# A two-layer hybrid transformer block on one core: the keys and queries of layer 2's attention are split a unit sooner, and the context's two attention units move into the small PSUM bank

## The chip, the core and the metric

The kernel runs on one core of a Trainium2 chip. Its time is the device time of one execution in microseconds (us); the median of three runs before is 3200.51 us (3197.03 to 3209.38). Five engines work side by side, each in its own order, and wait for each other through semaphores: TensorE (PE: matmuls and transposes, into the eight banks of PSUM), VectorE (DVE), ScalarE (ACT), GpSimd (POOL) and SyncE (SP), whose queue issues most transfers (DMA).

## The reference

Two layers run over 1024 latent tokens and 256 context tokens. Each layer has a convolution module, a retention part and multi-head attention side by side, one output projection, and a SwiGLU feed-forward part. The change touches attention alone. Shortened, with `l` the layer:

```python
def block_attention(q, k, v):                 # 8 heads, dq = 96, dv = 64
    ...
        s = jnp.einsum('bqhd,bkhd->bhqk', qi, k).astype(jnp.float32) * scale
        p = jax.nn.softmax(s, axis=-1).astype(v.dtype)
        return jnp.einsum('bhqk,bkhd->bqhd', p, v)
...
    attL = block_attention(qmL, jnp.concatenate([kmC, kmL], axis=1), jnp.concatenate([vmC, vmL], axis=1))
    ...
    if not last:
        attC = block_attention(qmC, kmC, vmC)
```

Latent queries (1024) read 1280 keys in both layers. Context queries (256) read the 256 context keys, and only in the first layer.

## The kernel before

**Units.** Attention of a layer is a loop over 8 heads `h` and two blocks `g` of 512 queries, each of four units `a` of 128 queries: 8 units a head, which the text numbers 0 to 7 (unit 8 is unit 0 of the next head). A unit's scores are nine matmuls into `S`, a PSUM tile of three banks of which there are two (`psum(S=2, po=1, mm=1)`): each operand is held as a rounded part and a rest (`kh`, `kl`, `qh`, `ql`), and three products replace one. DVE takes the negated row maximum `nm` (L994), ACT the exponentials `P` with their sums (L999), and DVE transposes `P` in blocks of 32 into `T1` (L1091). After a block's fourth unit, POOL (4 copies, L1026) and SP (12 DMAs, L1024) bring the 32-blocks of `T1` into place as `PT`.

**Weighing.** Five units later PE weighs the values with `PT` in four chunks, one a unit (`weigh_chunk`, L1037, into the bank `po`). With the last chunk it spreads the reciprocal sums over a tile of the one small bank `mm` (L1011), and `normalise` reads `po` and `mm`: two steps on ACT (L1049, L1051), one on DVE (`raw<-po,raw`) and one on POOL (`raw<-raw`).

**Context.** After unit 7 of a head (for the last head after unit 3) of layer 1, `context_units` computes two units of 128 context queries against 256 keys. Both write into one `S` tile, in different banks, each followed by its own maximum; then come two exponentials. A step later PE transposes them into `mm` (`direct_transposes`, L1064), ACT copies them out (L1069), another step later PE weighs them into `mm` (`direct_weigh`, L1075, L1011), and ACT and DVE finish (`od`).

**What sets the order.** The order on every engine is the order of the code. Two counters delay steps: `mids` ticks behind a unit's scores, `steps` at a unit's end; `later(d, f)` runs `f` at the d-th tick from now. What the work of a head needs is prepared during the head before: `load_head` (4 DMAs into the two `kq` tiles), `split_k` (ACT rounds `kh`, L877; POOL subtracts `kl`) and `split_q`, once for each block (`qh` on ACT, `ql` on POOL). Before, `split_k` runs at the end of unit 4, `split_q` of block 0 at the end of unit 5 and of block 1 at the end of unit 7, in both layers. The helper `mms` (L105) issues the products, `tt` (L80) every two-input step, so these go by tile names.

Of the kernel before, what the change touches and what calls it, by code (L numbers as in the profile page):

```python
# [11 lines left out]
F32 = mybir.dt.float32  # L12
# [4 lines left out]
AX = mybir.AxisListType  # L17
# [12 lines left out]
H_MLA = 8  # L30
# [13 lines left out]
def body(tc, I, out):  # L44
    nc = tc.nc
    mult, add, sub = ALU.mult, ALU.add, ALU.subtract

    def pool(name, bufs=1, space=None, side=None):
        kw = {}
        if space is not None:  # L50
            kw["space"] = space
        if side is not None:
            kw["side"] = side
        return tc.tile_pool(name=name, bufs=bufs, reuse_waits="tile", **kw)
# [6 lines left out]
    smp = es.enter_context(pool("small", 4))  # L61
# [14 lines left out]
    def bank(tag="mm", cols=512):  # L76
        return pools[tag].tile([128, cols], F32, name=tag, tag=tag)
# [25 lines left out]
    def mms(ps, xs, start=True, stop=True):  # L103
        for i, (a, b) in enumerate(xs):
            nc.tensor.matmul(ps, lhsT=a, rhs=b, start=start and i == 0, stop=stop and i == len(xs) - 1)  # L105
# [365 lines left out]
    with ExitStack() as st:  # L471
# [25 lines left out]
        A, S = modA[0, 0], modS[0, 0]  # L497
# [12 lines left out]
    for l in range(L):  # L510
        last = l == L - 1
# [453 lines left out]
        def split_wo(hf, kps, p=None):  # L965
            for kp in kps:
                wo_pcs[hf].append(piece(I["w_out"][l, hf, kp], leng=None if kp % 2 else nc.vector, p=p,
                                        raw=wo_raw.pop((hf, kp), None)))
# [15 lines left out]

        def scores(u, ps):

            nk = len(u.kts) * 128
            k0 = u.kts[0] * 128
            for c in range(0, nk, 512):
                n = min(512, nk - c)  # L990
                kc = slice(k0 + c, k0 + c + n)
                mms(ps[:, c:c + n], [(u.qh, u.hd.kh[:, kc]), (u.ql, u.hd.kh[:, kc]), (u.qh, u.hd.kl[:, kc])])
            u.nm = smp.tile([128, 1], F32, name="nm", tag="nm")
            nc.vector.reduce_max(out=u.nm, in_=ps[:, :nk], axis=AX.X, negate=True)  # L994
            u.ps = ps[:, :nk]

        def exponentials(u, P):

            nc.scalar.activation(out=P, in_=u.ps, func=AF.Exp, bias=u.nm, accum_out=u.sm)  # L999
            u.P = P  # L1000
# [87 lines left out]
        steps, mids, soon = Ticks(), Ticks(), []  # L1088
# [5 lines left out]
        def after(u, us, T1):  # L1094

            if T1 is None:
                return
            block_transpose(u, T1)
            if u is not us[-1]:
                return  # L1100
            blocks(us, T1)
            for i in range(len(CHUNKS)):
                mids.later(5 + i, weigh_chunk, us, i)
            steps.later(5, reciprocals, us)

        def late():
            while soon:
                f, *x = soon.pop(0)
                f(*x)

        def context_units(h):
            us = []
            rc = rawp.tile([128, 1024], F32, name="raw", tag="raw")
            ps = bank("S", 1536)
            sums = smp.tile([128, 4], F32, name="sums", tag="sums", bufs=6)
            for a in range(2):
                u = Unit()
                u.h, u.g, u.a, u.hd, u.kts, u.ending = h, 2, a * 128, heads[h], CTX, False
                u.qh, u.ql = (x[:, a * 128:a * 128 + 128] for x in qs[h, 2])
                u.sums, u.sm, u.t = sums, sums[:, a:a + 1], rc[:, 512:]  # L1120
                us.append(u)
                scores(u, ps[:, a * 512:])
            for a, u in enumerate(us):
                exponentials(u, rc[:, a * 256:a * 256 + 256])
            mids.later(1, direct_transposes, us)
            mids.later(2, direct_weigh, us)

        prev = None
        with tc.manual_schedule():
            for ti, (h, g) in enumerate(todo):  # L1130
                if ti == len(todo) - 1:
                    steps.later(E0, load_wo, 0, (0, 1))
                    steps.later(E1, split_wo, 0, (0, 1))
                    steps.later(E2, load_mixed, 0, 0)
                    steps.later(E2, load_mixed, 0, 1)
                    steps.later(E2, load_wo, 0, (2, 3))
                if g == 0:
                    if not last:
                        steps.later(1, split_q, h, 2)
                    if h:  # L1140
                        mids.later(1 if last else 2, load_v, h)
                    else:
                        steps.later(1, split_q, 0, 1)
                    if h < H_MLA - 1:
                        mids.later(1 if last else 2, load_head, h + 1)
                elif g == 1 and h < H_MLA - 1:
                    steps.later(1, split_k, h + 1)
                    steps.later(2, split_q, h + 1, 0)
                    steps.later(4, split_q, h + 1, 1)
                us = []  # L1150
                direct = ti == len(todo) - 1
                T1 = tp_.tile([128, 4, 4, 320], F32, name="T1", tag="T1")
                sums = smp.tile([128, 4], F32, name="sums", tag="sums", bufs=6)
                for a in range(4):
                    u = Unit()
                    u.h, u.g, u.a, u.hd, u.kts, u.ending = h, g, a * 128, heads[h], kvt, ti == len(todo) - 1
                    u.qh, u.ql = (x[:, a * 128:a * 128 + 128] for x in qs[h, g])
                    u.sums, u.sm = sums, sums[:, a:a + 1]
                    us.append(u)
                    if direct:  # L1160
                        P = T1.rearrange("p c u n -> p (c u n)")[:, a * NTOK:a * NTOK + NTOK]
                    else:
                        P = pp_.tile([128, NTOK], F32, name="P", tag="P")
                    scores(u, bank("S", 1536))
                    mids.tick()
                    exponentials(u, P)
                    if prev is not None:
                        after(*prev)
                    late()
                    prev = (u, us, None if direct else T1)  # L1170
                    if direct:
                        u.t = pp_.tile([128, NTOK], F32, name="P", tag="P")
                        mids.later(1 + a, direct_transposes, [u])
                        mids.later(3 + a, direct_weigh, [u])
                    if not last and a == 3 and g == (h < H_MLA - 1):
                        context_units(h)
                    steps.tick()
            while mids.q or steps.q or soon:
                mids.tick()
                late()  # L1180
                steps.tick()
            split_wo(0, (2, 3))
# [21 lines left out]
        def project_out(t, hf):  # L1204
            m_h, m_l = ms[t]
            ps = bank("mm")
            for k in range(KT):
                wh, wl = wo_pcs[hf][k // 2]
                c = slice((k % 2) * 512, (k % 2) * 512 + 512)
                mms(ps, [(m_h[:, k], wh[:, c]), (m_l[:, k], wh[:, c]), (m_h[:, k], wl[:, c])], k == 0, k == KT - 1)  # L1210
                if k % 2:
                    tk.tick()
                if k % 4 == 3:
                    next(todo, None)
            return ps
# [27 lines left out]
        for i, t in enumerate(order):  # L1243
            ps = [firsts.pop(t) if i < 2 else project_out(t, 0), project_out(t, 1)]
# [8 lines left out]
            u = (rawp if late else w2).tile([128, 1024], F32, name="raw" if late else "u", tag="raw" if late else "u")  # L1253
# [104 lines left out]
        steps = {}  # L1358
# [33 lines left out]
        for j in range(NJ):  # L1392
            v = steps.pop(j) if j in steps else first_two(j)
            w, x, u, th1 = v.w, feat.op, v.u, v.th
# [133 lines left out]
        while ahead:  # L1528
# [26 lines left out]
            for t in range(4):  # L1555
                ps = bank("po")
# [34 lines left out]
        for t in tiles:  # L1591
# [4 lines left out]
            ps = [bank("mm") for _ in range(2)]  # L1596
# [123 lines left out]
```

## Time and profile before

| | |
|---|---|
| median of 3 runs | 3200.51 us |
| the profiled execution, its own time | 3198.45 us |
| its span, first to last instruction | 3196.7 us |
| PE, DVE, POOL, ACT busy | 92%, 72%, 47%, 37% of the span |
| attention of layer 1, 446 to 712 us | 266 us, PE busy 234.15 us |
| attention of layer 2, 2130 to 2363 us | 233 us, PE busy 211.31 us |

PE is busy nearly all the time, and what it waits for is named in the view of waits. A row of the timeline gives start, duration, engine, line, operation, tile written and read, and in brackets the idle time of the engine before it with what ended it. A few gaps in a repeated loop are small one by one; they count by their number.

### The profile page before, as it was taken

The numbers are of one execution on the slowest core, as the hardware profiler recorded it, in microseconds if no ns is written. First come the engines' busy times: TensorE is split into PE (matmuls) and PEld (weight loads), VectorE is DVE, ScalarE is ACT, GpSimd is POOL, SyncE is SP. The second block draws the span as 40 slices with busy tenths as digits, with TensorE's granted clock in tenths as the row PEclk, the third lists the DMA queues.
The fourth block names the chain that finished last, engine by engine and source line by source line (L and its number), as shares of the span: only waits on it lengthen the run. The fifth ranks groups of instructions, "written<-read, shape, count | busy, mean of one in ns | idle before, by whom it ended". The sixth has DMA issues, their size and how long they took to land. (4 is left out here: it accounts for less than half of the span.)

```text
span 3196.7 us, 39725 instructions
## 1 busy us (share of the span) xinstructions
PE 2936.5 (92%) x13968; PEld 2271.7 (71%) x13968; DVE 2310.3 (72%) x3254; ACT 1196.4 (37%) x2354; POOL 1489.7 (47%) x1187
## 2 busy tenths in 40 slices
PE   7989989889879999999898898989999899999897
PEld 3667865557768888887776676865568678887675
DVE  4388467767897676655888868468856986666998
ACT  4213545553332222225332513545554332224432
POOL 1274535544432232325774365435644343334993
PEclk9989989999989999999999999999999999999998
DMA  7421157657522322213303421157764332224213
GB/s 278 141 67 34 58 178 182 167 129 255 198 81 98 105 91 91 91 65 138 112 20 109 152 66 48 44 184 178 180 181 155 99 113 86 86 81 154 96 66 119
DMA packets 178527, 381.47 MB, mean 119 GB/s; under 512 B 43255, under 2 KB 77687, under 8 KB 178072
## 3 DMA queue, kind: packets, MB, share of 16 engines
q1 hardware_dynamic: 172980, 360.03, 36.8%
q10 hardware_dynamic: 5348, 18.90, 1.4%
q8 instruction: 111, 1.82, 0.2%
q14 instruction: 88, 0.72, 0.1%
HBM read 242.97 MB, written 76.90 MB: 100 GB/s over the span
## 5 line engine op out<-in xcount | busy, mean ns | idle before, releaser
L80 POOL TENSOR_TENSOR wl<-raw,wh 128x512 fp32r<-128x512 f32 (+2 forms) x208 | 387.3, 1874 | 648.3 <-ACT wh L85 648.1
L85 ACT CAST wh<-raw 128x512 fp32r<-128x512 f32 (+2 forms) x305 | 237.6, 796 | 414.9 <-PE pp L105 190.1
L80 DVE TENSOR_TENSOR w<-pp,w 128x512 f32<-128x512 f32 x308 | 207.4, 686 | 186.2 <-PE pp L105 183.9
L994 DVE TENSOR_REDUCE nm<-S 128x1 f32<-128x1280 f32 (+1 forms) x144 | 196.3, 1363 | 89.4 <-PE S L105 87.9
L105 PE MATMUL po<-wh,gh 128*128 128x512 f32 x504 | 203.0, 403 | 35.8 <-DVE p L80 29.3
L999 ACT ACTIVATE P<-S,nm 128x1280 f32<-128x1280 f32 x120 | 159.4, 1329 | 196.6 <-DVE nm L994 196.6
L1026 POOL COPY PT<-T 32x1280 f32<-32x1280 f32 x120 | 150.0, 1250 | 177.3 <-PE mm L1011 116.6
L80 POOL TENSOR_TENSOR rr<-rv,mh 128x1 f32<-128x1 f32 (+2 forms) x130 | 93.1, 717 | 279.6 <-DVE rv L190 277.3
L105 PE MATMUL po<-wh,gl 128*128 128x512 f32 x504 | 200.1, 397 | 0.0
L105 PE MATMUL po<-wl,gh 128*128 128x512 f32 x504 | 199.5, 396 | 0.0
L584 DVE SCALAR_TENSOR_TENSOR cacc<-cy,cw,cacc 128x1295 f32<-128x1295 f32 (+1 forms) x120 | 193.7, 1655 | 0.0
L80 POOL TENSOR_TENSOR gl<-gr,gh 128x512 fp32r<-128x512 f32 x112 | 172.8, 1567 | 27.5 <-ACT gh L85 27.5
L80 POOL TENSOR_TENSOR wl<-sx,wh 128x1024 fp32r<-128x1024 f32 x44 | 109.5, 2488 | 155.9 <-ACT wh L85 155.9
L1091 DVE STREAM_TRANSPOSE T<-P 128x1280 f32<-128x1280 f32 x120 | 180.0, 1500 | 0.0
L1037 PE MATMUL po<-PT,vr 128*64 128x512 f32 x600 | 161.8, 636 | 9.6 <-POOL PT L1026 2.9
L80 DVE TENSOR_TENSOR raw<-raw 128x512 f32<-128x512 f32 (+1 forms) x96 | 127.5, 1336 | 50.5 <-POOL wl L80 47.6
L105 PE MATMUL S<-kh,qh 96*128 96x512 f32 (+1 forms) x384 | 154.3, 402 | 9.9 <-ACT P L999 8.2
L80 DVE TENSOR_TENSOR p<-p,po 128x512 f32<-128x512 f32 x224 | 145.3, 677 | 16.6 <-PE po L105 16.1
L105 PE MATMUL S<-kh,ql 96*128 96x512 f32 (+1 forms) x384 | 143.0, 372 | 9.2 <-POOL ql L80 9.2
L80 DVE TENSOR_TENSOR wl<-raw,wh 128x512 fp32r<-128x512 f32 (+1 forms) x105 | 125.3, 1202 | 28.0 <-ACT wh L85 27.9
L105 PEld LDWEIGHTS po<-wh,gh 128*128 128x128 f32 x504 | 96.9, 192 | 67.5 <-DVE p L80 34.9
L105 PE MATMUL S<-kl,qh 96*128 96x512 f32 (+1 forms) x384 | 142.6, 371 | 0.0
(437 smaller groups left out, 8703.7 us busy)
## 6 DMA issues: line engine op xcount, KB each, us to landing
PT<-T SPq DMA_DIRECT2D x360, 160.0 KB
raw<-in_mod_w SPq DMA_DIRECT2D x96, 512.0 KB
raw<-in_ffn_in SPq DMA_DIRECT2D x88, 512.0 KB
gd<-w SPq DMA_DIRECT2D x88, 256.0 KB
gr<-gd SPq DMA_DIRECT2D x32, 512.0 KB
xs<-x ACTq DMA_DIRECT2D x28, 512.0 KB
raw<-in_ffn_out SPq DMA_DIRECT2D x28, 512.0 KB
x<-xs SPq DMA_DIRECT2D x26, 512.0 KB
```

Of the source, the lines that this page charges most:

```text
L80: (eng or nc.vector).tensor_tensor(out=out, in0=a, in1=b, op=op)
L85: nc.scalar.copy(h, t)
L105: nc.tensor.matmul(ps, lhsT=a, rhs=b, start=start and i == 0, stop=stop and i == len(xs) - 1)
L584: nc.vector.scalar_tensor_tensor(out=acc[:, ct, :], in0=y0[:, ct, j:j + AW], scalar=w, in1=acc[:, ct, :], op0=mult, op1=add)
L994: nc.vector.reduce_max(out=u.nm, in_=ps[:, :nk], axis=AX.X, negate=True)
L999: nc.scalar.activation(out=P, in_=u.ps, func=AF.Exp, bias=u.nm, accum_out=u.sm)
L1026: nc.gpsimd.tensor_copy(o, i)
L1037: nc.tensor.matmul(u.po[64 * (j % 2):64 * (j % 2) + 64], lhsT=u.hd.v[:, j, :], rhs=src[:, :, j * 32:j * 32 + 32], start=j < 2, stop=j > 7)
L1091: nc.vector.transpose(out=T1[:, :, u.a // 128].rearrange("p c (k i) -> p k c i", i=32), in_=u.P.rearrange("p (k c i) -> p k c i", c=4, i=32))
```

## The change

The context's scores go into `mm` (one bank: 256 columns for each unit) in place of an `S` tile. The six products run without a maximum in between, and one DVE instruction takes both maxima (`nmc`). Context transposes and context weighing come one unit later. In layer 2 `split_k` and both `split_q` come one unit sooner: at the ends of units 3, 4 and 6. In layer 1 they stay at the ends of units 4, 5 and 7; they are only entered in the list earlier.

```diff
         def scores(u, ps):
 
+            score_products(u, ps)
+            nk = len(u.kts) * 128
+            u.nm = smp.tile([128, 1], F32, name="nm", tag="nm")
+            nc.vector.reduce_max(out=u.nm, in_=ps[:, :nk], axis=AX.X, negate=True)
+            u.ps = ps[:, :nk]
+
+        def score_products(u, ps):
             nk = len(u.kts) * 128
             k0 = u.kts[0] * 128
             for c in range(0, nk, 512):
                 n = min(512, nk - c)
                 kc = slice(k0 + c, k0 + c + n)
                 mms(ps[:, c:c + n], [(u.qh, u.hd.kh[:, kc]), (u.ql, u.hd.kh[:, kc]), (u.qh, u.hd.kl[:, kc])])
-            u.nm = smp.tile([128, 1], F32, name="nm", tag="nm")
-            nc.vector.reduce_max(out=u.nm, in_=ps[:, :nk], axis=AX.X, negate=True)
-            u.ps = ps[:, :nk]
...
             rc = rawp.tile([128, 1024], F32, name="raw", tag="raw")
-            ps = bank("S", 1536)
+            ps = bank("mm")
             sums = smp.tile([128, 4], F32, name="sums", tag="sums", bufs=6)
             for a in range(2):
...
                 us.append(u)
-                scores(u, ps[:, a * 512:])
+                u.ps = ps[:, a * 256:a * 256 + 256]
+                score_products(u, u.ps)
+            nm = smp.tile([128, 2], F32, name="nmc", tag="nmc")
+            nc.vector.reduce_max(out=nm, in_=ps.rearrange("p (a k) -> p a k", a=2), axis=AX.X, negate=True)
+            for a, u in enumerate(us):
+                u.nm = nm[:, a:a + 1]
             for a, u in enumerate(us):
                 exponentials(u, rc[:, a * 256:a * 256 + 256])
-            mids.later(1, direct_transposes, us)
-            mids.later(2, direct_weigh, us)
+            mids.later(2, direct_transposes, us)
+            mids.later(3, direct_weigh, us)
...
                     if h < H_MLA - 1:
                         mids.later(1 if last else 2, load_head, h + 1)
-                elif g == 1 and h < H_MLA - 1:
-                    steps.later(1, split_k, h + 1)
-                    steps.later(2, split_q, h + 1, 0)
-                    steps.later(4, split_q, h + 1, 1)
+                        steps.later(4 if last else 5, split_k, h + 1)
+                        steps.later(5 if last else 6, split_q, h + 1, 0)
+                        steps.later(7 if last else 8, split_q, h + 1, 1)
```

**PE in layer 1, between unit 7 and unit 8.** The rows run from the last weighing of unit 7 over the context's six products to the second product of unit 8; the names in brackets are the engines whose semaphores a row waits for. Before:

```order
L1037 MATMUL po<-PT,vr 64x512 x2
L105 MATMUL S<-kh,qch 128x256 [waits Activation_49]
L105 MATMUL S<-kh,qcl 128x256 [waits Pool_49]
L105 MATMUL S<-kl,qch 128x256
L105 MATMUL S<-kh,qch 128x256 [waits DVE_49]
L105 MATMUL S<-kh,qcl 128x256
L105 MATMUL S<-kl,qch 128x256
L105 MATMUL S<-kh,qh 128x512 [waits Activation_49]
L105 MATMUL S<-kh,ql 128x512 [waits Pool_49]
```

And now:

```order
L1041 MATMUL po<-PT,vr 64x512 x2
L105 MATMUL mm<-kh,qch 128x256
L105 MATMUL mm<-kh,qcl 128x256 [waits Pool_49]
L105 MATMUL mm<-kl,qch 128x256
L105 MATMUL mm<-kh,qch 128x256
L105 MATMUL mm<-kh,qcl 128x256
L105 MATMUL mm<-kl,qch 128x256
L105 MATMUL S<-kh,qh 128x512 [waits Activation_49]
L105 MATMUL S<-kh,ql 128x512 [waits Pool_49]
```

The wait for DVE between the two context units is gone, and so is that for ACT ahead of them; the wait for POOL in unit 8's second product stays.

**ACT in layer 1, from unit 8 to unit 10.** `P` is a unit's exponentials, `raw<-po` and `raw<-mm 64x256` are `normalise`, `raw<-mm 128x512` takes the context's transposes out of `mm`, `od<-mm` its weighed values. Before:

```order
L999 ACTIVATE P,sums<-S,nm 128x1280
L1049 COPY raw<-po 64x512
L1051 COPY raw<-mm 64x256 x2
L1069 COPY raw<-mm 128x512
L85 CAST qch<-kq 96x256
L999 ACTIVATE P,sums<-S,nm 128x1280
L1083 COPY od<-mm 64x256
```

And now:

```order
L1003 ACTIVATE P,sums<-S,nm 128x1280
L1053 COPY raw<-po 64x512
L1055 COPY raw<-mm 64x256 x2
L85 CAST qch<-kq 96x256
L1003 ACTIVATE P,sums<-S,nm 128x1280
L1073 COPY raw<-mm 128x512
L1003 ACTIVATE P,sums<-S,nm 128x1280
L1087 COPY od<-mm 64x256
```

The transposes' copy moved behind the exponentials of unit 9, the copy of `od` behind those of unit 10.

**POOL in layer 2, one head.** Before:

```order
L1026 COPY PT<-T_18482 32x1280 x4
L80 TENSOR_TENSOR raw<-raw 64x512
L80 TENSOR_TENSOR kl<-kq,kh 96x1280
L80 TENSOR_TENSOR ql<-kq,qh 96x512 x2
L1026 COPY PT<-T_18594 32x1280 x4
L80 TENSOR_TENSOR raw<-raw 64x512
```

And now:

```order
L80 TENSOR_TENSOR kl<-kq,kh 96x1280
L1030 COPY PT<-T_18466 32x1280 x4
L80 TENSOR_TENSOR raw<-raw 64x512
L80 TENSOR_TENSOR ql<-kq,qh 96x512 x2
L1030 COPY PT<-T_18582 32x1280 x4
L80 TENSOR_TENSOR raw<-raw 64x512
```

`kl` stands ahead of block 0's copies now; both `ql` stay between the blocks. In layer 1 POOL's order is as it was.

## Rows read from the trace of the kernel before

**Rows 1.** Windows: length; busy us of PE, PEld, DVE, ACT, POOL; granted clock; DMA.

```profile
446.00:712.00 266.00, 234.15 (x1120) 148.26 (x1121) 199.17 (x184) 141.47 (x246) 136.14 (x103) 0.94 0.64 157
...
545.51:578.59 33.08, 28.93 (x148) 17.73 (x150) 25.91 (x24) 18.32 (x32) 18.63 (x15) 1.00 0.70 169
578.59:613.59 35.00, 32.17 (x148) 19.27 (x150) 25.91 (x24) 18.32 (x32) 18.65 (x15) 0.90 0.66 160
...
2180.64:2193.01 12.37, 10.49 (x40) 5.66 (x42) 6.58 (x6) 4.73 (x9) 6.78 (x5) 0.72 0.28 65
2299.52:2310.28 10.76, 9.00 (x40) 5.18 (x42) 6.59 (x7) 4.72 (x9) 5.99 (x5) 0.84 0.31 73
2242.80:2251.09 8.29, 7.44 (x38) 4.17 (x38) 6.51 (x7) 4.68 (x9) 4.61 (x5) 1.00 0.31 73
```

**Rows 2.** Waits of PE in layer 1's attention: us in total, times, longest.

```profile
PE S L105 <- DVE nm L994: 14.6, 8, 2.4
PE mm L1064 <- ACT raw L1051: 11.7, 7, 2.2
```

**Rows 3.** Timeline, layer 1, from unit 7 of a head to unit 9.

```profile
566.98 0.39 PE L105 MATMUL S<-kh,qch 96*128 96x256 f32 x1
...
568.05 1.26 POOL L80 TENSOR_TENSOR ql<-kq,qh 96x512 fp32r<-96x512 f32 x1
...
569.35 0.39 PE L105 MATMUL S<-kh,qch 96*128 96x256 f32 x1 [1.75 <-DVE nm L994]
...
570.04 0.39 PE L105 MATMUL S<-kh,ql 96*128 96x512 f32 x1
...
571.62 1.94 PE L1037 MATMUL po<-PT,vr 128*64 128x512 f32 x8
571.73 1.49 DVE L994 TENSOR_REDUCE nm<-S 128x1 f32<-128x1280 f32 x1 [1.29 <-PE S L105]
...
575.37 0.68 DVE L80 TENSOR_TENSOR raw<-po,raw 64x512 f32<-64x512 f32 x1 [0.73 <-ACT raw L1049]
...
576.16 0.66 PE L1064 MATMUL mm<-ident,raw 128*128 128x128 f32 x4 [2.17 <-ACT raw L1051]
576.57 0.47 PE L105 MATMUL S<-kh,qh 96*128 96x512 f32 x1
```

**Rows 4.** Groups by shape, layer 1's attention: busy us, mean ns | idle before.

```profile
L999 ACT ACTIVATE P<-S,nm 128x1280 f32<-128x1280 f32 x60 | 79.7, 1328 | 97.1 <-DVE nm L994 97.1
...
L999 ACT ACTIVATE raw<-S,nm 128x256 f32<-128x256 f32 x16 | 7.4, 470 | 12.2 <-DVE nm L994 12.2
...
L994 DVE TENSOR_REDUCE nm<-S 128x1 f32<-128x256 f32 x16 | 6.5, 405 | 6.5 <-PE S L105 6.5
```

**Rows 5.** Timeline, layer 1, the first head's split of `ql`.

```profile
471.53 1.27 POOL L80 TENSOR_TENSOR ql<-kq,qh 96x512 fp32r<-96x512 f32 x1
```

**Rows 6.** Waits of PE in layer 2's attention.

```profile
PE S L105 <- POOL ql L80: 9.2, 6, 2.6
```

**Rows 7.** Timeline of PE in layer 2: the three longest of them.

```profile
2155.80 0.80 PE L105 MATMUL S<-kh,ql 96*128 96x512 f32 x1 [2.62 <-POOL ql L80]
2183.92 0.79 PE L105 MATMUL S<-kh,ql 96*128 96x512 f32 x1 [1.88 <-POOL ql L80]
...
2302.68 0.52 PE L105 MATMUL S<-kh,ql 96*128 96x512 f32 x1 [1.76 <-POOL ql L80]
```

**Rows 8.** Timeline of layer 2, one head's chain to `ql`.

```profile
2228.25 1.49 DVE L994 TENSOR_REDUCE nm<-S 128x1 f32<-128x1280 f32 x1
...
2234.23 5.17 POOL L1026 COPY PT<-T 32x1280 f32<-32x1280 f32 x4 [6.81 <-PE mm L1011]
2235.48 1.26 ACT L877 CAST kh<-kq 96x1280 fp32r<-96x1280 f32 x1
...
2240.70 2.95 POOL L80 TENSOR_TENSOR kl<-kq,kh 96x1280 fp32r<-96x1280 f32 x1
...
2243.60 1.28 POOL L80 TENSOR_TENSOR ql<-kq,qh 96x512 fp32r<-96x512 f32 x1
```

## The prediction, written before the changed kernel was run

> **What bounds the kernel now.** I read the page first: PE is busy 92% of the span, so time is to be had where PE idles or runs at its lower clock. The windows of the two attention stretches come next. In layer 1's, 266 us long, PE is busy 234.15, and its mean granted clock is 0.94 [rows 1]. No other engine is near full there (DVE 199, ACT 141, POOL 136), so PE's order and PE's waits set the pace. The view of waits names them: 14.6 us in 8 waits for DVE's maximum, one behind each first context unit, and 11.7 us in 7 waits for ACT's copies out of `mm`, ahead of the context's transposes [rows 2]. Together that is 26.3 us. In layer 2 the first entry is 9.2 us in 6 waits for POOL's `ql`, at the start of a head [rows 6]. These three entries are what the change aims at. The reader should then look in the timeline for what stands right behind each of them, because a removed wait only gives what the next one leaves.
>
> **Layer 1, the context's scores.** The six products stay, at the same length; they only change their bank. Take the head in rows 3. Before, the first context product starts at 566.98, the second unit's at 569.35 after 1.75 us of waiting, and unit 8's second product, which reads `ql`, starts at 570.04 [rows 3]. Without the wait it would be asked for at 570.04 - 1.75 = 568.29. But POOL ends that `ql` at 568.05 + 1.26 = 569.31, and POOL's order in layer 1 is unchanged. So the product starts at about 569.35, 0.69 us sooner than before, with a new wait of 1.06 us for POOL. Of 1.75 us only 0.69 is won in such a head. There are six of them (heads 0 to 6 have a successor, and the first is different). In the first head `ql` ends at 471.53 + 1.27 = 472.80 [rows 5], about when PE came to it anyway: nothing won. The last head has no successor and no `ql`: there the whole 1.75.
>
> Two maxima become one, `nmc`, of 512 columns. No row shows that form. Two of the old ones took 2 x 0.405 us [rows 4]; one over 1280 columns takes 1.49 [rows 3], so by columns 512 would be 0.405 + 256 x (1.49 - 0.405) / 1024 = 0.68. I take 0.68, with 0.4 and 0.81 as ends; DVE idles 1.29 us in front of unit 8's maximum [rows 3], which covers either. On the other side nothing is added to ACT: the same two exponentials.
>
> **Layer 1, the step later.** Before, the transposes at 576.16 wait 2.17 us, because the weights of the block before lie in `mm` until `normalise` has copied them, and unit 9's scores stand behind them at 576.57 [rows 3]. Now unit 9's scores come first, and the wait goes: with the 0.69, PE reaches them at 576.16 - 2.17 - 0.69 = 573.30. What is late next? Unit 9's weighing needs the bank `po`, free when DVE's sum ends: 575.37 + 0.68 - 0.69 = 575.36 [rows 3]. PE comes there after unit 9's scores; unit 8's, with the second context unit ahead, took 571.62 - 569.35 = 2.27, of which about 0.45 was the context (the 0.69 from 569.35 to 570.04 less one of unit 8's products), so 1.82 to 1.9: at 575.2. A wait of 0.2 us. The transposes themselves then find `mm` copied out. Their 0.4 us (576.57 - 576.16), and the context's weighing, are moved by a unit, not removed. Their readers on ACT move behind the exponentials of the next unit, 1.33 us each [rows 4], and PE comes a full unit later too. So 2.17 - 0.2 = 1.97 per head.
>
> A steady head thus wins 0.69 + 1.97 = 2.66, six heads 16.0. The last wins 1.75 + 2.17 - 0.2 = 3.7, as its waits are like the others'. Layer 1: **19.7 us** of the 26.3.
>
> **Layer 2, the splits.** The chain in rows 8: POOL copies `PT` from 2234.23, then come `normalise`'s step, `kl` (2.95 us) and `ql`, done at 2243.60 + 1.28 = 2244.88. Now `kl` goes ahead of the copies. It needs `kh`: the maximum of unit 3 ends at 2228.25 + 1.49 = 2229.74, its exponentials and their sum take 1.33 + 0.2, `kh` 1.26, so `kh` is there at 2232.5 and `kl` ends at 2235.5 [rows 4, 8]. POOL was idle 6.81 us before its copies, which hides `kl` but for 1.27 us; the copies start that much later. `ql` ends 2.95 - 1.27 = 1.68 us sooner. The six waits shrink by up to 1.68: the three longest, 2.62, 1.88 and 1.76 [rows 7], leave 0.94, 0.20 and 0.08; the other three make 9.2 - 6.26 = 2.94 together, and I take them as gone. 9.2 - 1.2 = **8.0 us**. The copies of block 0 are needed five units later, so 1.27 us costs nothing. No DMA is added or moved; `load_head` is issued at the same place, some four units ahead of the earlier `split_k`. On ACT, `kh` stands between the exponentials of units 3 and 4, where ACT has about 1.3 us free (a unit of 2.9 less 1.33 and 0.2): equal to `kh`'s 1.26, so at worst 0.1 us.
>
> **The clock.** [...] The head from 578.59 took 35.00 us at 0.90, the one before it 33.08 at 1.00, with the same work and the same kind of waits [rows 1]: 1.9 us, and the next head looks alike. In layer 2 the windows behind the waits of 1.88 and 1.76 show 0.72 and 0.84; PE is busy 10.49 and 9.00 for what takes 7.44 at 1.00 [rows 1, 7]: 3.05 and 1.56. Together 3.9 + 4.6 = 8.5 us that waits may have cost on top. With the waits shortened I take 5 of them; the ends are 0 and 8.5. [...]
>
> **The sum.** 19.7 + 8.0 + 5 = 32.7, about 33 us. The profiled execution took 3198.45 us (2.06 below the median of 3200.51); 33 less gives 3165.5, and on the median **3167.5 us**.
>
> **Rivals.**
> - *Everything goes.* The remaining wait for `ql` is not there, and the clock stays up: 26.3 + 9.2 + 8.5 = 44, so 3156.5. Against it: POOL's unchanged order in layer 1, and 569.31 in rows 3.
> - *The step later costs what it wins.* The transposes' copy stands behind unit 9's exponentials, and if PE then waits for it before the context weighing, half of the 1.97 goes in seven heads, 7 us, and the clock gives nothing: 3200.5 - (27.7 - 7) = 3180. For it: every step of this part runs through the single bank `mm`, whose wait is the one in rows 2.
> - *Hardly anything.* POOL's chain to `ql` binds a head of layer 1 more tightly than I read, by 2 us a head, so that layer 1 gives 4 and layer 2 its 8: 3188.5. This is also the case in which the splits, sooner by the diff, are held by something else.
> - *Slower: the small bank becomes the chain.* With the scores in `mm`, the weights of the old block (behind the weighing at 571.62, sooner by 0.69, 1.94 long: at 572.9) cannot be written before ACT has taken the context's exponentials. `nmc` ends at about 569.7 and two exponentials of 0.47 and their sums run to 570.9 [rows 3, 4]: 2.0 us to spare. If they came 2.0 us later than that PE would begin to lose; only at about 2.0 + 2.66 + 1.0 (layer 2's 8.0 over eight) = 5.7 us is all gain gone, and 8 us give 3200.5 + 8 x 2.3 = 3219. [...]
>
> **How the numbers follow.** Forecast 0.62 (3164 to 3173, as the clock gives all or nothing); everything 0.09; step later 0.18; hardly anything 0.08; slower 0.03. The range reaches from below the "everything" case to above the "step later" case: 3153 to 3186. About 0.5%, 16 us, is what a measurement here can tell from no change: faster than that, below 3184.5, is 0.62 + 0.09 + 0.15 = 0.86; within it 0.11 (0.08 and the upper edge of the third case); slower 0.03.
>
> **What would show it.** In layer 1's waits the entry for DVE's maximum is gone, that of the transposes on ACT near zero, and a new one, PE on POOL's `ql`, stands at 6 times about 1.1 us and once some 3 us (first head); with it small waits on DVE's `raw`. A steady head takes about 30.4 us where it took 33.08. In layer 2 the entry for `ql` falls from 9.2 to between 1 and 2 us, `kl` stands before `PT` on POOL, and the windows from unit 8 show 1.00. I am wrong if the transposes still wait in their new place, if the weights (L1015 in the new file) wait for ACT, if `kh` delays ACT's exponentials in layer 2, or if the clock falls as often as before.

## The result and the profile after

The changed kernel took 3164.58 us (median of 4 runs, 3158.51 to 3171.39); the kernel before, beside it on the same chip, 3204.95 (3197.03 to 3211.34). The ratio is 0.988, 95% interval 0.986 to 0.990: about 40 us less, faster by more than 0.5%. The prediction subtracted from 3200.51, the median of the three runs that there were then; against that it is 36 us less. The prediction was 3167.5 us, within 3153 to 3186. A second set of runs of the same kernel, called after_again below, gave 3164.13.

Where the time went is read from stretches that run from DVE's row maximum for a layer's first full unit to that for its last. A head is such a stretch from the maximum of its unit 0 to that of the next head's; heads 2 to 6 of layer 1, which repeat the same work, are called steady. First the kernel before, by windows (length; busy us of PE, of its weight loads PEld, of DVE, ACT and POOL, each with its instructions; mean granted clock, where 1.00 is full speed and 0.50 half of it; DMA's busy share and GB/s): layer 1 and layer 2. A steady head at 1.00 and one with a fall of the clock, cut at another place of the head, stand in [rows 1].

```profile
448.27:709.69 261.42, 229.79 (x1095) 144.74 (x1095) 197.68 (x183) 140.51 (x244) 136.14 (x103) 0.94 0.64 157
2132.81:2360.25 227.44, 206.44 (x951) 124.51 (x951) 186.94 (x151) 123.27 (x188) 130.63 (x95) 0.95 0.74 174
```

The same stretches of the changed kernel: layer 1, layer 2, a steady head of layer 1 (all five are 30.54 to 30.57 us long, at 1.00), and a later head of layer 2.

```profile
451.57:689.40 237.83, 221.28 (x1095) 139.83 (x1095) 195.44 (x176) 139.83 (x244) 136.03 (x103) 0.98 0.70 172
2110.18:2324.97 214.79, 208.19 (x951) 127.93 (x951) 187.66 (x151) 123.21 (x188) 130.55 (x95) 0.94 0.78 184
537.85:568.42 30.57, 29.00 (x148) 17.68 (x150) 25.62 (x23) 18.22 (x32) 18.63 (x14) 1.00 0.74 183
...
2244.99:2272.17 27.18, 26.61 (x130) 15.54 (x132) 24.58 (x20) 16.17 (x25) 17.93 (x13) 1.00 0.84 200
```

Layer 1 lost 23.6 us and layer 2 12.7. The instructions of PE are the same in number, so the columns divide the gain. In layer 1 PE's idle time fell from 261.42 - 229.79 = 31.6 to 16.6 us, by 15.1, and its busy time by 8.5: that is the clock, 0.94 before and 0.98 after. In layer 2 idle time fell from 21.0 to 6.6 us, by 14.4, and busy time rose by 1.75; a half clock in its first two heads (0.50 for 27.31 us) moves time from the one to the other there, which the part on why the prediction was right takes up. What lies between, ahead of and behind the two stretches gave 1.5 us; the change does not touch it.

Two of PE's waits in the changed kernel's layer 1 (us in total, times, longest), against [rows 2]:

```profile
PE S L105 <- POOL ql L80: 10.8, 7, 3.6
...
PE po L1041 <- DVE raw L80: 1.2, 7, 0.2
```

Both entries of [rows 2] are gone. The new first one is the wait that the prediction put there. The timeline around one of them, from the context's first product to unit 9 (start, duration, engine, line, operation; in brackets idle time and what ended it), answers to [rows 3]:

```profile
564.18 0.39 PE L105 MATMUL mm<-kh,qch 96*128 96x256 f32 x1
...
565.28 1.27 POOL L80 TENSOR_TENSOR ql<-kq,qh 96x512 fp32r<-96x512 f32 x1
...
566.12 0.65 DVE L1129 TENSOR_REDUCE nmc<-mm 128x2 f32<-128x512 f32 x1
566.61 0.50 PE L105 MATMUL S<-kh,ql 96*128 96x512 f32 x1 [1.21 <-POOL ql L80]
...
572.07 0.68 DVE L80 TENSOR_TENSOR raw<-po,raw 64x512 f32<-64x512 f32 x1 [0.74 <-ACT raw L1053]
...
572.80 1.08 PE L1041 MATMUL po<-PT,vr 128*64 128x512 f32 x4 [0.16 <-DVE raw L80]
573.81 0.66 PE L1068 MATMUL mm<-ident,raw 128*128 128x128 f32 x4
...
574.23 0.48 PE L105 MATMUL S<-kh,qh 96*128 96x512 f32 x1
```

PE runs the context's six products without a pause, asks for `ql`, and has to wait until POOL ends it at 566.55. The transposes at 573.81 wait for nothing. The weighing ahead of them waits 0.16 us for `po`.

In layer 2 the entry for `ql`, 9.2 us in [rows 6], is down to one of 0.2 (1.9 us in two waits in the profile of after_again). POOL's order there, against [rows 8]:

```profile
2205.28 2.94 POOL L80 TENSOR_TENSOR kl<-kq,kh 96x1280 fp32r<-96x1280 f32 x1 [5.11 <-issue]
...
2208.18 5.17 POOL L1030 COPY PT<-T 32x1280 f32<-32x1280 f32 x4
...
2214.68 2.53 POOL L80 TENSOR_TENSOR ql<-kq,qh 96x512 fp32r<-96x512 f32 x2
```

`kl` runs where POOL had been idle, ahead of the copies.

### The profile page after: what moved, and what is told of

It reads as the page before. It is cut to its first block, busy times and chain, and to the rows that moved or that the text cites. A ratio compares the mean times of both kernels' runs of the same rounds, so it can differ in the third digit from the quotient of the medians.

```text
span 3158.9 us, 39704 instructions
## 1 busy us (share of the span) xinstructions
PE 2932.1 (93%) x13968; PEld 2275.9 (72%) x13968; DVE 2306.9 (73%) x3246; ACT 1194.4 (38%) x2354; POOL 1490.8 (47%) x1187
## 5 line engine op out<-in xcount | busy, mean ns | idle before, releaser
L990 DVE TENSOR_REDUCE nm<-S 128x1 f32<-128x1280 f32 x128 | 189.7, 1482 | 56.1 <-PE S L105 54.7
L80 POOL TENSOR_TENSOR gl<-gr,gh 128x512 fp32r<-128x512 f32 x112 | 173.9, 1577 | 27.5 <-ACT gh L85 25.8
L80 DVE TENSOR_TENSOR p<-p,po 128x512 f32<-128x512 f32 x224 | 145.3, 677 | 16.6 <-PE po L105 16.1
```

The lines of the kernel that those rows point to most:

```text
L80: (eng or nc.vector).tensor_tensor(out=out, in0=a, in1=b, op=op)
```

## The experiments

Each run below changes one thing, and its layers are compared by the same stretches, layer 1 and layer 2, as above. The part in between, which none of them touches, took 1421 to 1440 us in these profiles; so differences of a few us between total times say less than differences between stretches.

**The two halves of the change.** splits_only is the kernel before with the new places of `split_k` and `split_q`; context_only is the changed kernel with the old ones:

```diff
-                        steps.later(4 if last else 5, split_k, h + 1)
-                        steps.later(5 if last else 6, split_q, h + 1, 0)
-                        steps.later(7 if last else 8, split_q, h + 1, 1)
+                elif g == 1 and h < H_MLA - 1:
+                    steps.later(1, split_k, h + 1)
+                    steps.later(2, split_q, h + 1, 0)
+                    steps.later(4, split_q, h + 1, 1)
```

> The kernel before with only layer 2's splits a unit sooner; the context is as it was. My account (the gain is three separate parts, each worth its waits): layer 1 stays at some 261 us from the first unit's maximum to the last, layer 2 falls from 227 to about 215 us, PE's waits for POOL's ql there from 9.2 us to under 1; 8 to 13 us less than before (ratio about 0.997). Rival (it is the fallen clock that pays, and it comes back by chance): no more than 3 us less, or a gain that appears in layer 1 as well.

Measured: 3186.46 us, ratio 0.9956 (0.9943 to 0.9969), 15.9 us less than the kernel before in its set. Layer 2 took 215.0 us (227.4 before), layer 1 262.1 (261.4).

> The changed kernel with the splits of both layers entered as before. My account: layer 1 as in the changed kernel, about 238 us between its first and last maximum, layer 2 as before, 227 us, with some 9 us of waits for ql; 22 to 28 us less than before (ratio about 0.992), so that this part and the splits alone add up to the whole, 37 to 40 us. Rival (the parts help each other): the two alone give clearly less, under 30 us together.

Measured: 3174.81 us, ratio 0.9918 (0.9903 to 0.9934), 27.5 us less. Layer 1 took 237.2 us, layer 2 229.7. The windows of layer 1 and layer 2 of context_only:

```profile
448.49:685.72 237.23, 221.03 (x1095) 139.74 (x1095) 195.38 (x175) 139.90 (x244) 136.10 (x103) 0.98 0.70 172
2117.11:2346.85 229.74, 212.67 (x951) 129.74 (x951) 187.54 (x151) 123.26 (x188) 130.63 (x95) 0.92 0.72 172
```

Each half works in its own layer alone. By the medians their gains, 15.9 and 27.5, add up to 43 where the whole gave 40; by the ratios they are about 14 and 26, 40 together. That the splits' half was worth more than the 8 to 13 us expected is not shown: its interval is about 10 to 18 us, and its layer 2 lost 12.5.

**The context's half, taken apart.** no_step_later keeps the small bank and the one maximum, but transposes and weighs a unit earlier, as before:

```diff
-            mids.later(2, direct_transposes, us)
-            mids.later(3, direct_weigh, us)
+            mids.later(1, direct_transposes, us)
+            mids.later(2, direct_weigh, us)
```

> The changed kernel, but the context's transposes and weighing where they were, one unit sooner. My account: PE waits again about 2 us in each of 7 heads for ACT's copies out of the small bank ahead of the transposes, 12 to 16 us more than the changed kernel; a steady head of layer 1 goes from 30.6 to about 32.6 us. Rival (the shared bank and the one maximum alone remove the wait, because unit 8 comes sooner): 0 to 4 us more.

Measured: 3185.19 us, ratio 0.995 (0.9936 to 0.9963). Layer 1 took 258.6 us, 2.8 less than the kernel before. One of its PE waits in layer 1:

```profile
PE mm L1068 <- ACT raw L1055: 15.2, 7, 2.2
```

The wait ahead of the transposes is back, and it costs more than its length. Its windows of layer 1 and of a steady head:

```profile
444.81:703.43 258.62, 226.58 (x1095) 142.75 (x1095) 196.27 (x175) 140.40 (x244) 135.92 (x103) 0.95 0.65 158
566.81:600.90 34.09, 30.51 (x148) 18.60 (x150) 25.75 (x24) 18.30 (x32) 18.59 (x14) 0.95 0.68 164
```

Layer 1 is 20.8 us above the changed kernel's: 15.5 are idle time of PE (258.62 - 226.58 against 16.55), the other 5.3 are busy time. Where the changed kernel's heads run at 1.00, this one is at 0.95, with PE busy 1.5 us longer for the same products; the two behind it are alike, 34.1 us each.

two_maxima keeps the small bank and the step later, but takes one maximum behind each context unit:

```diff
-                score_products(u, u.ps)
-            nm = smp.tile([128, 2], F32, name="nmc", tag="nmc")
-            nc.vector.reduce_max(out=nm, in_=ps.rearrange("p (a k) -> p a k", a=2), axis=AX.X, negate=True)
-            for a, u in enumerate(us):
-                u.nm = nm[:, a:a + 1]
+                scores(u, u.ps)
```

> The changed kernel, but each context unit has its own maximum right behind its products, in the small bank. My account (what was won at this place is the wait between the two units, not the bank): the second unit waits for the first maximum again, 1.75 us a head, the wait for ql disappears behind it, 0.7 us a head net and 1.75 in the last: layer 1 some 6 us longer than in the changed kernel, about 243. Rival (the S tile that is no longer taken is what was won): as the changed kernel, within 1 us in layer 1.

Measured: 3177.51 us, ratio 0.9917 (0.9899 to 0.9935); layer 1 256.2 us, 18 above the changed kernel where 6 was expected. One wait of PE, one case of it in the timeline, and the windows of layer 1 and of a steady head:

```profile
PE mm L105 <- DVE nm L990: 15.7, 8, 3.4
```

```profile
568.23 0.58 PE L105 MATMUL mm<-kh,qch 96*128 96x256 f32 x1 [1.75 <-DVE nm L990]
```

```profile
447.90:704.08 256.18, 234.41 (x1095) 147.34 (x1095) 197.07 (x184) 139.79 (x244) 135.84 (x103) 0.92 0.66 160
538.52:572.48 33.96, 32.01 (x148) 19.46 (x150) 25.89 (x25) 18.21 (x32) 18.59 (x15) 0.90 0.67 165
```

The pause of 1.75 us between the two context units is back though the bank is the new one. So it is the maximum between them, not the bank, that makes it. Of the 18 us 5.2 are idle time (21.77 against 16.55), about what was expected of the waits, and 13.1 are busy time: the clock falls in the steady heads, here to 0.90.

later_only is the kernel before with the step later alone, 2 and 3 in place of 1 and 2:

```diff
-            mids.later(1, direct_transposes, us)
-            mids.later(2, direct_weigh, us)
+            mids.later(2, direct_transposes, us)
+            mids.later(3, direct_weigh, us)
```

> The kernel before, with the context's transposes and weighing one unit later and nothing else; scores stay in an S tile with two maxima. My account: the wait for ACT's copies ahead of the transposes (11.7 us) goes, the 14.6 us behind the first maximum stay; layer 1 13 to 18 us shorter, about 246. Rival (the step later pays only once the scores are out of the S tiles, since unit 9 then waits for the context's S tile): under 6 us shorter, with a wait of unit 9's scores for ACT.

Measured: 3199.63 us, ratio 0.9983 (0.9971 to 0.9995). Layer 1 took 260.0 us, 1.4 less than before, though the transposes' wait is gone; the context's weighing waits once for ACT, 0.3 us. One of its PE waits, then the windows of layer 1 and of a steady head, then those of the pause in it and of what follows, from the second context unit to unit 9's first product:

```profile
PE S L105 <- DVE nm L994: 14.4, 8, 2.1
```

```profile
445.37:705.34 259.97, 239.32 (x1095) 149.11 (x1095) 197.28 (x183) 139.64 (x244) 135.87 (x103) 0.90 0.64 157
537.68:571.77 34.09, 32.13 (x148) 19.24 (x150) 25.89 (x25) 18.20 (x32) 18.56 (x15) 0.90 0.68 164
```

```profile
564.66:568.05 3.39, 1.64 (x9) 0.62 (x8) 3.29 (x4) 1.59 (x4) 3.34 (x2) 1.00 0.81 228
568.05:575.87 7.82, 7.82 (x28) 4.42 (x29) 3.33 (x3) 3.42 (x8) 1.72 (x2) 0.56 0.00 0
```

Before 568.05 PE was busy 1.64 of 3.39 us, at the full clock. Behind the pause it ran 7.82 us without a gap at a mean of 0.56. Against the kernel before, PE's idle time in layer 1 fell from 31.6 to 20.7 us, by 11.0, and its busy time rose from 229.8 to 239.3, by 9.5. The gain of the step later was there, and the clock took most of it back.

**Is it the pause that lowers the clock?** Up to here that is only a coincidence in place. later_fill is later_only with useless work in the pause: PE repeats the first context unit's three products five times into the free small bank, which nobody reads.

```diff
...
                 scores(u, ps[:, a * 512:])
+                if a == 0:
+                    fill = bank("mm")
+                    for i in range(FILL):
+                        score_fill(u, fill[:, i % 2 * 256:i % 2 * 256 + 256])
```

> The kernel before with the step later alone, plus 15 more products in each head: between the context's two units PE repeats the first unit's three products five times into the free small bank, where in later_only it stands idle for 1.75 us. Nothing reads them. They are 15 x 0.117 = 1.75 us of PE work, so the second unit cannot start sooner than in later_only; all that goes is the pause. Theory (the pause makes PE's clock fall right behind it, which took the gain of the step later back): the heads of layer 1 fall from 34.1 us to between 30.7 and 32 (34.1 less up to 3.4 of half-clock time), the slow-clock time of the stretch from 51 us to under 25, the stretch from 260 to 240-250 us, the median to 3183-3192. Rival (the falls have another cause, or the lower clock only shows time that PE has to spare): heads stay within 0.5 us of 34.1, stretch 258-262, median 3198-3202. A second rival (the wait is only shifted: DVE's maximum comes later as the added products hold PE's semaphore): a wait of PE behind the added products of 0.5 us or more, heads over 34.1.

Measured: 3179.79 us, ratio 0.9935 (0.9918 to 0.9952), 22.4 us less than the kernel before in its set, where later_only gave 5.3 in its own, and that with 120 products more. Layer 1 took 242.1 us in place of 260.0. Its windows of layer 1, of a steady head, and of the stretch from the second context unit to unit 9's first product:

```profile
448.14:690.29 242.15, 234.42 (x1215) 153.30 (x1215) 196.63 (x184) 139.78 (x244) 136.26 (x103) 0.99 0.69 169
534.55:565.64 31.09, 30.73 (x163) 19.52 (x165) 25.77 (x25) 18.22 (x33) 18.63 (x14) 1.00 0.75 180
```

```profile
563.24:567.84 4.60, 4.60 (x30) 2.89 (x29) 2.62 (x3) 2.14 (x6) 1.27 (x2) 1.00 0.00 0
```

The last stretch is the same work as the 7.82 us row of later_only. It takes 4.60 us at 1.00: 3.2 us less, and the whole head is 34.1 - 31.1 = 3.0 us shorter. Nothing else was changed in PE's order, so the pause of 1.75 us is what the falls of later_only hang on. The head's 31.09 us is also what the prediction's working gives for the step later by itself: 33.08 [rows 1] less 1.97 is 31.11.

**Layer 1's splits a unit sooner, too.** The change leaves layer 1's splits at units 4, 5 and 7. splits_both moves them as in layer 2:

```diff
-                        steps.later(4 if last else 5, split_k, h + 1)
-                        steps.later(5 if last else 6, split_q, h + 1, 0)
-                        steps.later(7 if last else 8, split_q, h + 1, 1)
+                        steps.later(4, split_k, h + 1)
+                        steps.later(5, split_q, h + 1, 0)
+                        steps.later(7, split_q, h + 1, 1)
```

> The changed kernel with the splits a unit sooner in layer 1 as well. My account: ql comes some 1.6 us sooner, so the 1.2 us waits for it go, but kh is asked for before its keys have landed (in the changed kernel they land 1 us after kh's place at the latest, a unit sooner is 3 us before that), ACT stands for some 3 us a head in front of unit 4's exponentials, and PE loses up to 1.2 us in units 5 and 6: layer 1 between 234 and 243 us. Rival (POOL's chain is all that counts): layer 1 at 230 us or less, as with ql on VectorE.

Measured: 3195.41 us, ratio 0.997 (0.9957 to 0.9983). Layer 1 took 265.2 us, 27 above the changed kernel; layer 2, where nothing differs, 212.1. That is far above the 243 us at most that were expected. The waits for `ql` are gone, and a worse one has come. A wait of PE, the window of layer 1, and the timeline of one case:

```profile
PE po L1041 <- issue: 23.5, 6, 4.5
```

```profile
450.06:715.30 265.24, 239.08 (x1095) 151.62 (x1095) 195.81 (x175) 139.66 (x244) 135.66 (x103) 0.88 0.63 154
```

```profile
563.75 1.26 ACT L877 CAST kh<-kq 96x1280 fp32r<-96x1280 f32 x1 [4.01 <-DMA kq<-krd]
564.92 1.32 ACT L1003 ACTIVATE P<-S,nm 128x1280 f32<-128x1280 f32 x1
...
566.35 0.58 ACT L1053 COPY raw<-po 64x512 f32<-64x512 f32 x1
...
566.97 0.68 DVE L80 TENSOR_TENSOR raw<-po,raw 64x512 f32<-64x512 f32 x1 [4.38 <-ACT raw L1053]
...
567.75 1.97 PE L1041 MATMUL po<-PT,vr 128*64 128x512 f32 x4 [3.85 <-issue]
```

ACT reaches the rounding of `kh` before the next head's keys have landed and stands still for 4.01 us. The exponentials, then the copy out of `po`, then DVE's sum stand behind it in order, and PE's weighing needs the `po` that this sum frees. "issue" in the last row is a wait whose end the view does not name; the row above it ends 0.1 us earlier at 567.65, and that is how I read it. Of the 27 us only 9.6 are idle time of PE (26.16 against 16.55); 17.8 are busy time, at a granted clock of 0.88 in place of 0.98. So layer 1's place of the splits is bounded on both sides: a unit sooner and the keys are not there, as it is and `ql` is 1.2 us late.

**What comes after the wait for `ql`.** ql_on_dve gives block 0's `ql` of layer 1 to DVE:

```diff
-                        steps.later(5 if last else 6, split_q, h + 1, 0)
+                        steps.later(5 if last else 6, split_q, h + 1, 0, None if last else nc.vector)
```

> The changed kernel, but in layer 1 the rest ql of a head's first block is subtracted on VectorE (0.7 us) and not behind kl on POOL. My account (POOL's chain to ql is what is left of the removed wait): the 7 waits for ql, 10.8 us in the changed kernel, go but for 2 us in the first head, and the time falls by 7 to 9 us; a steady head takes about 29.4 us. Rival (kl, which ends 1.3 us before ql, or VectorE's own queue holds PE as long): 0 to 2 us less, with a wait for kl or for the maximum in the same place.

Measured: 3160.46 us, ratio 0.988 (0.9861 to 0.9899). Layer 1 took 231.6 us, 6.2 less than the changed kernel; no wait for `ql` is left, and the one for `po` grew:

```profile
PE po L1041 <- DVE raw L80: 3.5, 7, 0.6
```

kl_in_two leaves the work on POOL, but subtracts `kl` of layer 1 in two pieces, 512 keys ahead of `ql` and 768 behind it:

```diff
-            tt(u.kl, u.k, u.kh, sub, leng or nc.gpsimd)
+            n = NTOK if first is None else first
+            tt(u.kl[:, :n], u.k[:, :n], u.kh[:, :n], sub, leng or nc.gpsimd)
+
+        def split_k_rest(h, first):
+            u = heads[h]
+            tt(u.kl[:, first:], u.k[:, first:], u.kh[:, first:], sub, nc.gpsimd)
...
-                        steps.later(4 if last else 5, split_k, h + 1)
+                        steps.later(4 if last else 5, split_k, h + 1, None, None, None if last else 512)
                         steps.later(5 if last else 6, split_q, h + 1, 0)
+                        if not last:
+                            steps.later(6, split_k_rest, h + 1, 512)
```

> The changed kernel, but in layer 1 POOL subtracts kl in two pieces, the first 512 keys ahead of block 0's ql and the other 768 behind it, so that ql is there some 1.7 us sooner (kl takes 2.94 us for 1280 columns, so about 1.2 for 512 and 1.75 for 768). Theory (the wait of 1.2 us per head for POOL's ql is the last one of its kind, and only POOL's order sets it): the wait goes in six heads, a small one for po or for kl's second piece (up to 0.4) takes its place, steady heads fall from 30.55 to 29.4-29.9 us, the stretch from 238 to 231-234, the median 4-7 us below the changed kernel's: 3157-3160. Rival (the cost of a further POOL instruction, or kl's second piece, needed by the sixth product of the unit, is late by as much): heads within 0.3 of 30.55, the wait named kl instead of ql, median 3163-3166.

Measured: 3157.14 us, ratio 0.9861 (0.9844 to 0.9879), the lowest time of all. Layer 1 took 231.8 us, steady heads 29.8. The first wait of PE in layer 1, and a steady head:

```profile
PE S L105 <- POOL kl L80: 2.4, 6, 0.4
```

```profile
564.24:594.03 29.79, 29.08 (x148) 17.59 (x150) 25.62 (x23) 18.20 (x33) 18.79 (x15) 1.00 0.77 188
```

Both kernels show that POOL's order was the next limit, worth some 6 us in layer 1. In total time their intervals overlap with the changed kernel's. A second set of runs of the changed kernel, in which nothing differs:

> The changed kernel once more, beside its variants on the same chip. Both accounts: 0.988 of the kernel before, layer 1 some 238 us between first and last maximum, layer 2 some 215; what differs from its first profile lies in the stretches that the change does not touch, by the clock.

Measured: 3164.13 us, ratio 0.9874 (0.9851 to 0.9898), layer 1 238.0 and layer 2 212.5 us. The two profiles of the same kernel differ by 0.1 us in layer 1, by 2.3 in layer 2 and by some 11 us in the untouched part between. So kl_in_two is 6.0 us better by its stretch, and by the total likely, not certainly, better.

## Why the prediction was right

*The context's scores.* Of the 1.75 us of waiting 0.69 was to be won, with a new wait of 1.06 for `ql`. Measured: 1.21 at 566.61, and 3.6 once in the first head (1.9 in after_again), where some 3 had been written down. `nmc` took 0.65 us (0.68 taken). Here the prediction looked past the removed wait and read what POOL would hold back; without that step it would have said 1.75 a head.

*The step later.* 2.17 - 0.2 was to be won, and a wait for `po` of 0.2 to appear. Measured: 0.16 in the head shown, 1.2 us in seven heads, and no wait ahead of the transposes. By itself at the full clock it gave 33.08 - 31.09 = 1.99 (later_fill) where 1.97 was taken.

*The steady head.* 30.4 us predicted, 30.57 measured at 1.00. This term is 2.5 in place of 2.66.

*Layer 1's sum.* 19.7 us of waits was too much: PE's idle time fell by 15.1. The prediction won 1.97 at the transposes in each of seven heads, 13.8 us, where [rows 2] has 11.7 for this wait in all. Four of the seven waits are 2.2 us long; the other three are 1.14, 0.85 and 1.02, in heads where the mean clock from the second context unit to that wait was 0.73, 0.57 and 0.56. One of the three, in the kernel before:

```profile
611.17 0.66 PE L1064 MATMUL mm<-ident,raw 128*128 128x128 f32 x4 [0.85 <-ACT raw L1051]
```

The second context unit of that head starts at 602.43. At that mean of 0.57 PE asks for the transposes 7.9 us behind it (611.17 - 0.85 - 602.43), where in [rows 3], at 1.00, it asks after 4.6 (576.16 - 2.17 - 569.35). So a part of what was counted as waiting was there as busy time, and it was won as such: the clock gave 8.5 us of PE's busy time in layer 1.

*Layer 2.* 8.0 was taken. In the changed kernel's profile the entry for `ql` fell by 9.0 and PE's idle time by 14.4, but in that profile's first two heads PE ran at half clock, 0.50, for 27.31 of 52.89 us, and its longer busy time there (51.16 us, 43.02 in after_again) fills what would be waits. The profile of after_again, of the same kernel, has less of it. Windows of the first two heads and of the other six, in the order before, changed kernel, after_again:

```profile
2132.81:2187.10 54.29, 44.38 (x186) 30.09 (x186) 44.90 (x35) 28.76 (x42) 28.36 (x20) 0.87 0.61 149
2187.10:2360.25 173.15, 162.06 (x767) 94.42 (x769) 142.04 (x117) 94.51 (x146) 102.27 (x75) 0.97 0.78 182
...
2110.18:2163.07 52.89, 51.16 (x186) 35.41 (x186) 45.84 (x34) 28.75 (x42) 28.35 (x20) 0.74 0.63 152
2163.07:2324.97 161.90, 157.03 (x767) 92.53 (x769) 141.83 (x117) 94.46 (x146) 102.20 (x75) 1.00 0.82 195
...
2119.42:2170.23 50.81, 43.02 (x186) 28.75 (x186) 45.24 (x34) 28.74 (x42) 28.30 (x20) 0.93 0.65 158
2170.23:2331.91 161.68, 157.06 (x767) 92.50 (x769) 141.81 (x117) 94.44 (x146) 102.19 (x75) 1.00 0.82 195
```

Waits of PE in layer 2, in the same order (for before, the entry for `ql` is [rows 6]):

```profile
PE S L105 <- ACT P L999: 5.0, 5, 1.3
...
PE S L105 <- ACT P L1003: 1.3, 1, 1.3
PE S L105 <- POOL ql L80: 0.2, 1, 0.2
...
PE S L105 <- ACT P L1003: 5.7, 6, 1.3
PE S L105 <- POOL ql L80: 1.9, 2, 1.7
```

In after_again PE's idle time is 12.4 us, 8.6 less than before, and 1.9 us of waits for `ql` are left where the prediction left 1.2. The waits for the exponentials are not smaller there than before; they are so only where the half clock covers them. So the term for the waits held, 8.6 for 8.0. What layer 2 gave on top is the clock: in the six heads behind the second PE was busy 162.06 us before at 0.97, and 157.03 and 157.06 after at 1.00.

`kh` on ACT, which was to cost 0.1 us at worst, shows no cost: a later head is 27.18 us long with PE busy 26.61 of it.

*The clock.* This is the step that was treated most loosely: 5 us for both layers, with ends of 0 and 8.5. Measured were 8.5 in layer 1 and 5.0 in layer 2's six later heads, 13.5 together, outside these ends. One reason is the price. The prediction compared the lengths of a head at 1.00 and one at 0.90, 1.9 us apart; PE's busy time in them is 3.2 us apart (32.17 and 28.93, [rows 1]), and the wait ahead of the transposes, 2.17 us in the one and 0.85 in the other, hid the rest. And the falls hang on the pauses: in later_only the clock took back 9.5 us of the 11.0 that the removed wait gave, and in no_step_later and two_maxima it added 5.3 and 13.1 us to a wait put back. The changed kernel's steady heads, where no pause is over 1.21 us, all ran at 1.00. With one of 1.75 or 2.17 left, the clock fell in the steady heads of the three kernels: 0.90 in later_only and two_maxima, 0.95 in no_step_later. The kernel before stood in between, with a pause of 1.75 us in a head at 1.00 and in one at 0.90 [rows 1]. So here a pause of that length went with a fall in some heads and not in others.

In sum the prediction's 33 stands against 37.8 by the two profiles (23.6, 12.7 and 1.5) and 40 by the two medians. The direction of every step held. The waits in layer 1 were over-sized by 4.6 us, the clock was under-sized by 8.5 (13.5 for 5), and the half clock in layer 2's first two heads, which no step foresaw, took back a part: they are 2.1 us longer than in after_again. That the total came so near is partly luck, as these errors have opposite signs.

*The rivals.* "Everything goes" fell with the 10.8 us for `ql`. "The step later costs what it wins" fell as neither the transposes nor the context's weighing wait for `mm`. "Hardly anything" fell in layer 1 by the steady head. The slower case, the small bank as the chain, fell as well: the spreading of the reciprocal sums into `mm` (L1015) has no entry in the waits, though `mm` has one user more.

## What to carry to other kernels

When a wait is to be removed, read in the timeline what is ready right behind it, on which engine, and count only the difference; that gave each of the steady head's numbers here to 0.2 us. Count it in each head by itself: a steady head's gain times the number of heads was more than the whole entry. Then look at what the clock does with the pause that is left: two changes that each remove one of two pauses in a loop can be worth little alone and much together (in layer 1, 1.4 us in later_only and 2.8 in no_step_later, 23.6 with both). Moving a preparing step sooner has an end where its input lands: in splits_both ACT stood still 4.01 us for the keys, and held all that was queued behind it.

## What was not expected of the hardware

**A pause cost more than its length, and useless work repaid it.** 15 products added in a pause of 1.75 us shortened each steady head by 3.0 us, as the granted clock stayed at 1.00 in place of 0.90.

**Heads of one length.** In later_only and no_step_later the steady heads behind the first are 34.0 to 34.1 us long, though the pauses in them differ (1.75 us in the one, 1.2 and 2.17 in the other) and so do their mean clocks (0.90 and 0.95). The waits don't explain why they agree so closely; no run here tells why, and it stays open.

**A half clock that cost little.** In the changed kernel's layer 2 PE ran at half clock, 0.50, for 27.31 us without a gap:

```profile
2115.11:2142.42 27.31, 27.31 (x73) 20.57 (x73) 23.33 (x17) 13.51 (x19) 14.37 (x11) 0.50 0.67 153
```

Over the first two heads PE was busy 51.16 us, where it was busy 43.02 in after_again, 8.1 less for the same work; yet the two heads took only 2.1 us more (52.89 and 50.81). The rest went into time in which PE waited in after_again. So most of this low clock hid in a stretch where PE had time to spare, and its busy share, 51.16 of 52.89 us, said little of the time. The code is the same in both profiles; why this stretch began at half clock in one of them stays open.
